# One plain copy of the transposed weights in place of a split into two rounded parts, in the second layer's attention

## The chip, the cores and the metric

The kernel runs on one core of a Trainium2 chip. The metric is the device time of one execution in microseconds (us), lower is better. A core has TensorE for matmuls (PE in the profile; its weight loads are listed as PEld), VectorE (DVE), ScalarE (ACT), GpSimd (POOL) and SyncE (SP), which here only starts DMAs. Matmuls write to PSUM banks; DVE and ACT read them.

## The reference, cut to what matters

The model is a two-layer decoder trunk over 1024 tokens of width 1024, all in float32. The first layer (A) has a sparse attention with three branches, the second (B) a dilated attention over shared keys and values; both end in a SwiGLU. The change is in layer B:

```python
DILATIONS = ((128, 1), (512, 4), (2048, 16))

def banded_attention(q, k, v, max_dist, dist_scale, rel_bias):
    ...
    s = jnp.einsum('nbqgrd,nbkgd->nbgrqk', qb, kw).astype(jnp.float32) * dh ** -0.5
    ...
    p, denom, m = masked_softmax(s + bias, mask[None, :, None, None])
    o = jnp.einsum('nbgrqk,nbkgd->nbqgrd', p, vw.astype(jnp.float32))
    o = o / denom[..., 0].transpose(0, 1, 4, 2, 3)[..., None]
    lse = (jnp.log(denom) + m)[..., 0].transpose(0, 1, 4, 2, 3).reshape(n, L, G, R)
    return o.reshape(n, L, G, R, dh), lse

def dilated_attention(h, w_q, k_shared, v_shared, w_out, rel_bias):
    q = (h @ w_q).reshape(B, S, N_DIL, N_KV, GQA_R, HEAD_DIM)
    ...  # one banded attention for each of the three dilations
    alpha = jax.nn.softmax(jnp.stack(lses, axis=-1), axis=-1)
    o = jnp.einsum('bsgrdi,bsgri->bsgrd', jnp.stack(outs, axis=-1), alpha)
    return o.reshape(B, S, D_MODEL).astype(h.dtype) @ w_out
```

There are 16 heads of 64 columns in 4 groups; the four heads of a group share their keys and values.

## The kernel before, in words

The program runs stage after stage: projections and attention of layer A, its output projection and feed-forward part, the projection of layer B's queries and of the shared keys and values (`project_B`), layer B's attention, and layer B's output projection and feed-forward part with the final norm. Within a stage, the order of the instructions in each engine's queue is set by a planner that simulates a timeline when the program is built; `after(...)` fixes single pairs. Each engine then takes its queue in order and waits on semaphores.

Numbers that need more than TensorE's quick rounded format (`F32R`, "fp32r" in the profile) are split: a rounded part on ACT (`split`, L165) and the rest on DVE (L166). A product of two such pairs takes two or three rounded matmuls. A matmul of two plain float32 operands needs no split.

`project_B` computes V for each of the three dilations, transposes it with TensorE, splits it, and stores for each token tile and group 128 columns: 64 of the rounded part and 64 of the rest (`vBs`). The stores are started by POOL.

Layer B's attention loops over the four groups. For each, `wide_job` is made for 8 residues r and two pairs of heads (hp 0 and 1): 64 units in all that do the dilations 4 and 16 together, with three blocks of 128 keys. `near_job` is made for 8 tiles t of 128 queries and two pairs: 64 units for dilation 1, with two blocks of keys (one at t = 0). Each is a `unit`. Its front part computes for the two heads e of its pair the scores into an `s` bank (L1672 and L1677, or L1692), adds the bias on DVE (L1638, with the row's minimum) and takes the exponential on ACT (L1643) into P. Its back part, `back`, is issued two units later (`pipelined(jobs(), 2)`): for at most two blocks at a time it transposes the weights of both heads into a `pt` bank (`transposed`, L328), brings them to SBUF, and multiplies them with V into an `o` bank (`mm_pv`). There are three `s`, three `pt` and two `o` banks.

How the transposed weights leave the `pt` bank differs before the change. Mostly they are split into th on ACT (L165) and tl on DVE (L166), 512 columns at a time. The third block of a wide unit (`pick`) is copied as traw by ACT for hp 0 and by DVE for hp 1 (L340), and split by POOL (L341, L342). For hp 1 of near units with an even tile (`unsplit`), the plain copy of ACT (L332) is used as it is.

`mm_pv` takes all 128 columns of V as weights, so the output rows 0 to 63 hold the product with V's rounded part and the rows 64 to 127 that with the rest, for 2 x 128 columns, the queries of the two heads. With th and tl these are two rounded matmuls (L348, L349) for each block; with traw it is one plain matmul (L347), of which the profile lists two records. After the second pair, `evac_o` adds the two halves: for each e, ACT copies one half of the rows (L359) and DVE adds the other to it (L360), and head e lands on the rows 64 e to 64 e + 63 of its destination, which is `o12` for wide units (every eighth column) and `oT` for near ones.

`merge` weighs and adds the two results of a group with small transposes (L1707, L1713, L1735) and matmuls with `crow` (L1742, L1743, L1744), spread between the units of the next stretch.

Of the kernel before, what the change touches and what calls it, by code (L numbers as in the profile page):

```python
# [10 lines left out]
F32 = mybir.dt.float32  # L11
F32R = mybir.dt.float32r
# [9 lines left out]
NT = S // 128  # L22
KC = D // 128
H = 16
G = 4
DH = 64
# [89 lines left out]
def trunk(ctx, tc, I, out):  # L116
    nc = tc.nc
# [7 lines left out]
    f32 = lambda ap: ap.bitcast(F32)  # L125
# [3 lines left out]
    dram = pool(ctx, "dram", space=DR)  # L129
# [10 lines left out]
    def bank(name):  # L140
        return psum[name].tile([128, 512], F32, name=name, bufs=BANKS.get(name, 1))
# [6 lines left out]
    ident = cst.tile([128, 128], F32, name="ident")  # L148
# [13 lines left out]
    def split(H_, L_, src, scale=None, eng=None):  # L162

        if scale is None:
            prev = nc.scalar.activation(H_, src, AF.Copy)  # L165
            rest = (eng or nc.vector).tensor_sub(L_, src, f32(H_))  # L166
            (on_vector if eng is None else on_pool)[0] = rest
        else:
            prev = nc.scalar.activation(H_, src, AF.Copy, scale=scale)
            nc.vector.scalar_tensor_tensor(L_, src, scale, f32(H_), op0=OP.mult, op1=OP.subtract)  # L170
        return prev
# [173 lines left out]
    def mm_pv(o_, v, th, tl, cs, first, last):  # L345
        if tl is None:
            return nc.tensor.matmul(o_, f32(v), th[:, cs], start=first, stop=last, skip_group_check=True)  # L347
        nc.tensor.matmul(o_, v, th[:, cs], start=first, stop=False, skip_group_check=True)  # L348
        return nc.tensor.matmul(o_, v, tl[:, cs], start=False, stop=last, skip_group_check=True)  # L349

    cp_a, cp_v = nc.scalar.copy, nc.vector.tensor_copy

    def evac_o(p, po, dst):

        ov = po[:].rearrange("p (c e q) -> p c e q", e=2, q=128)
        tmp = p.tile([128, 2, 128], F32, name="ot", bufs=2)
        for e in range(2):
            own, oth = slice(64 * e, 64 * e + 64), slice(64 - 64 * e, 128 - 64 * e)
            nc.scalar.activation(tmp[own], ov[oth, :, e, :], AF.Copy)  # L359
            nc.vector.tensor_add(dst[own], ov[own, :, e, :], tmp[own])  # L360
# [1027 lines left out]
    xS = dram.tile([S, D], F32, name="xS")  # L1388
    qB = dram.tile([3, H, 128, S], F32, name="qB")
    kBs = dram.tile([3, G, 2, DH, S], F32, name="kBs")  # L1390
    vBs = dram.tile([3, NT, 128, G, 128], F32, name="vBs")
    second = ("T1", "T2", "T3", "T4", "B22")

    def dense(layer, w, x_src, oT, tail, near, far):
# [29 lines left out]
    def project_B(c, B, xr, scratch):  # L1424
# [51 lines left out]
        def tokens_out(n):  # L1476

            i = jobs[n][1]
            got = {}

            def done(a, r, C):
                got[a, r] = C
                if (a, r) == (1, 0):
                    got[a, r] = (place if i == 2 else lambda x: x)(own("x1"))
                    nc.scalar.activation(got[a, r], view_of(n)(C[:]), AF.Copy)
                if (a, r) != (1, 1):
                    return
                banks = Turns(["dx0", "dx1", "dx2", "dx3"])
                for t in range(NT):
                    if i == 0:  # L1490
                        hf, cols = t // 4, lambda x: x[:, (t % 4) * 128:(t % 4 + 1) * 128]
                    elif i == 1:
                        hf, cols = t % 2, lambda x: x[:, t // 2:512:4]
                    else:
                        hf = t % 2
                        cols = lambda x: x.rearrange("p j r -> p r j")[:, t - hf:t - hf + 2, :] \
                            .rearrange("p r j -> p (r j)")
                    pt = bank(banks())
                    for s in range(2):
                        nc.tensor.transpose(pt[:, s * 128:(s + 1) * 128], cols(got[s, hf]), ident)  # L1500
                    vt = vts().bitcast(F32R).rearrange("p (g d) -> p g d", d=128)
                    split(vt[:, :, 0:64], vt[:, :, 64:128], pt[:, :256].rearrange("p (g d) -> p g d", d=64))
                    if i < 2:
                        nc.gpsimd.dma_start(vBs[i, t], f32(vt))
                    else:
                        for s in range(2):
                            nc.gpsimd.dma_start(vBs[i, t - hf + s, hf * 64:(hf + 1) * 64],
                                                f32(vt[s * 64:(s + 1) * 64]))
            return done

        def view_of(n):
# [45 lines left out]
    with ExitStack() as c:  # L1557
# [10 lines left out]
                nc.scalar.activation(crow[:, a * 512:(a + 1) * 512], rs_f, AF.Copy, scale=0.0)  # L1568
        rQ = [Ring(f"Q{i}", [128, S], F32R, [(bB if i == 0 else bA, 4)]) for i in range(3)]
        rK = [Ring(f"K{i}", [128, S], F32R, [(bB if i == 0 else bA, 2)]) for i in range(3)]  # L1570
        rV = [Ring(f"V{i}", [128, NT, 128], F32R, [(bB if i == 0 else bA, 1)]) for i in range(3)]
        rT0 = Ring("T0", [128, 256], F32, [(bB, 5)])
        rT12 = Ring("T12", [128, 384], F32, [(bA, 4), (bB, 4)])
        grp = {}
# [1 line left out]
        def load_first():  # L1576

            T = {}
            for i in (1, 2):
                T[i] = grp[i, 0] = [rQ[i].tile() for _ in range(4)], [rK[i].tile() for _ in range(2)], rV[i].tile()  # L1580
            for lo, hi in ((0, 256), (256, 512), (512, 1024)):
                for i in (1, 2):
                    Q, K, V = T[i]
                    for hh in range(4):
                        nc.sync.dma_start(f32(Q[hh][:, lo:hi]), qB[i, hh][:, lo:hi])
                    if hi > 512 and i == 1:
                        continue
                    ks = slice(2 * lo, 2 * hi) if i == 1 else slice(lo + 128 * (lo > 0), min(hi + 128, S))
                    for z in range(2):
                        for b in range(2):  # L1590
                            nc.sync.dma_start(f32(K[z][b * 64:(b + 1) * 64, ks]), kBs[i, 0, z][:, ks])
                    vs = slice(ks.start // 128, ks.stop // 128)
                    nc.sync.dma_start(f32(V[:, vs]), vBs[i, vs, :, 0, :].rearrange("t p d -> p t d"))

        def load(i, g):
            Q = [rQ[i].tile() for _ in range(4)]
            K = [rK[i].tile() for _ in range(2)]
            V = rV[i].tile()
            for hh in range(4):
                nc.sync.dma_start(f32(Q[hh]), qB[i, 4 * g + hh])  # L1600
                if hh == 0:
                    for z in range(2):
                        load_k(K[z], kBs[i, g, z])
            nc.sync.dma_start(f32(V), vBs[i, :, :, g, :].rearrange("t p d -> p t d"))
            grp[i, g] = Q, K, V

        def load_T12(g, e):
# [17 lines left out]

        po_ = {}

        pick = lambda hp, b0, nb: (cp_a, cp_v)[hp] if nb == 3 and b0 == 2 else None
        unsplit = lambda key, hp: key[1] == 0 and hp == 1 and key[2] % 2 == 0

        def unit(key, hp, stats, slot, score, bias, n, blocks, dst):

            P = wk.tile([128, 2, 384], F32, name="P", bufs=4)
            for e in range(2):
                hh = 2 * hp + e
                ps = bank("s")
                score(ps, hh)
                nc.vector.tensor_tensor_reduce(out=P[:, e, :n], in0=ps[:, :n], in1=bias(hh), scale=1.0,  # L1638
                                               scalar=3e38, op0=OP.add, op1=OP.min,
                                               accum_out=stats[:, slot, hh:hh + 1])  # L1640
            for e in range(2):
                hh = 2 * hp + e
                nc.scalar.activation(P[:, e, :n], P[:, e, :n], AF.Exp, bias=stats[:, slot, hh:hh + 1], scale=-1.0,  # L1643
                                     accum_out=stats[:, slot, 4 + hh:5 + hh])

            def back():
                if hp == 0:
                    po_[key] = bank("o"), None
                po, prev = po_[key]
                nb = len(blocks)  # L1650
                for b0 in range(0, nb, 2):
                    bs = range(b0, min(b0 + 2, nb))
                    th, tl = transposed(wk, [P[:, e, b * 128:(b + 1) * 128] for b in bs for e in range(2)],
                                        pick(hp, b0, nb), 5, unsplit(key, hp))
                    for i, b in enumerate(bs):
                        cs = slice(i * 256, (i + 1) * 256)
                        o_ = po[:, hp * 256:(hp + 1) * 256]
                        with after(prev if b == 0 else None):
                            prev = mm_pv(o_, blocks[b], th, tl, cs, b == 0, b == nb - 1)
                po_[key] = po, prev  # L1660
                if hp == 1:
                    evac_o(wk, po, dst)
            return back

        def wide_job(g, r, hp):
# [178 lines left out]
```

## Time and profile before

| | |
|---|---|
| three runs | 2938.28 us median, 2936.68 to 2944.49 |
| the profiled execution | 2938.84 us, of which its span is 2937.1 |
| granted TensorE clock over the span | 0.989 |
| PE busy | 2816.6 us (96%) |
| DVE busy | 2398.0 us (82%) |
| ACT busy | 1621.1 us (55%) |
| POOL busy | 1642.7 us (56%) |
| layer B's attention | about 1857 to 2180 us of the span |

A row of a group has line, engine, operation, out and in by the program's names, shapes, and the count; then the busy time in us with the mean of one in ns; then the idle time of the engine just before, and what ended it ("<-"; "issue" where nothing that the profile shows was waited for). A row of the timeline has the start and the length in us. Matmuls are pipelined: a matmul's length includes the way through the array and out of it, and the next starts before its end. A shape such as 128*64 with 128x64 stands for 128 rows and 64 columns of weights and 64 columns that stream through. A row of the table by stretches gives each engine's busy time and count, the granted clock, and the share of the DMA engines.

### The profile page before, as it was taken

The page shows a single profiled execution, that of the slowest core. Times are in us where ns is not written, and L with a number is a line of the kernel's source. Part 1 is how long each engine was busy: PE and PEld are TensorE (multiplying, and loading weights), DVE is VectorE, ACT ScalarE, POOL GpSimd, SP SyncE. Part 2 cuts the span into 40 slices and gives each one's busy share as a digit, 9 for nine tenths or more (in the row PEclk, how much of TensorE's full clock was granted, in tenths as well). Part 3 has the DMA queues.
Part 4 walks back from the last instruction along what each step waited for, and adds up shares of the span by engine and source line. Part 5 has one row for each costly group of instructions (what it writes and reads, how often), then busy time and mean ns, then how long its engine had stood idle before and what let it go on. Part 6 is the DMA issues. An engine that isn't in the chain of part 4 may idle for free. (4 is left out here: it accounts for less than half of the span.)

```text
span 2937.1 us, 44584 instructions
## 1 busy us (share of the span) xinstructions
PE 2816.6 (96%) x14734; PEld 2375.5 (81%) x14734; DVE 2398.0 (82%) x4866; ACT 1621.1 (55%) x3615; POOL 1642.7 (56%) x1727
## 2 busy tenths in 40 slices
PE   9999999999999999999999999899989999999997
PEld 8888888887778888888777778788867788888886
DVE  5543988988888989989976777699998788888887
ACT  5432988887563433334454444699975543343334
POOL 3135766765566556556547777444425655666562
PEclk9999999999999999999999999999999999999999
DMA  8678132112322222231225555865431211112112
GB/s 255 212 240 296 34 105 82 44 47 80 108 62 65 71 73 69 62 85 52 84 85 153 155 162 148 278 201 164 136 136 52 69 57 59 58 47 65 54 44 76
DMA packets 277319, 317.59 MB, mean 108 GB/s; under 512 B 19196, under 2 KB 210733, under 8 KB 277088
## 3 DMA queue, kind: packets, MB, share of 16 engines
q1 hardware_dynamic: 255344, 246.50, 27.8%
q0 software_dynamic: 21744, 68.23, 7.4%
q8 instruction: 117, 1.92, 0.3%
q14 instruction: 114, 0.93, 0.1%
HBM read 243.17 MB, written 87.20 MB: 112 GB/s over the span
## 5 line engine op out<-in xcount | busy, mean ns | idle before, releaser
L885 DVE TENSOR_TENSOR pl<-oT,ph 128x512 fp32r<-128x512 f32 x337 | 350.8, 1058 | 57.5 <-PE dr L934 17.4
L884 ACT ACTIVATE ph<-oT 128x512 fp32r<-128x512 f32 x347 | 210.9, 626 | 203.7 <-PE ux L1082 54.6
L328 PE MATMUL pt<-ident,P 128*128 128x128 f32 x1536 | 243.7, 276 | 11.0 <-DVE tl L166 5.3
L166 DVE TENSOR_TENSOR tl<-pt,th 128x512 fp32r<-128x512 f32 (+1 forms) x336 | 217.5, 653 | 27.2 <-ACT th L165 25.7
L884 ACT ACTIVATE ph<-oTb 128x512 fp32r<-128x512 f32 x239 | 145.6, 627 | 170.4 <-PE ux L1082 52.9
L885 DVE TENSOR_TENSOR pl<-oTb,ph 128x512 fp32r<-128x512 f32 x233 | 213.2, 937 | 28.9 <-PE dr L934 17.4
L939 DVE TENSOR_TENSOR xr<-xr,dr 128x512 f32<-128x512 f32 x320 | 204.0, 679 | 15.9 <-PE dr L934 15.4
L803 POOL TENSOR_SCALAR P<-P,sm,gates 128x384 f32<-128x384 f32 (+7 forms) x256 | 183.4, 728 | 44.8 <-DVE sm L801 39.7
L939 DVE TENSOR_TENSOR xr<-xr,dx 128x512 f32<-128x512 f32 x320 | 204.6, 678 | 1.9 <-PE dx L934 1.9
L165 ACT ACTIVATE th<-pt 128x512 fp32r<-128x512 f32 (+1 forms) x336 | 185.6, 565 | 35.6 <-PE pt L328 31.0
L328 PEld LDWEIGHTS pt<-ident,P 128*128 128x128 f32 x1536 | 178.7, 141 | 32.0 <-DVE tl L166 5.3
L1266 POOL TENSOR_TENSOR oT<-oT,gffn 128x512 f32<-128x512 f32 x92 | 113.5, 1244 | 139.7 <-DMA oT<-in_ffn_w_up_dram 101.8
L799 ACT ACTIVATE P<-P,m 128x384 f32<-128x384 f32 (+7 forms) x256 | 170.7, 669 | 9.0 <-DVE m L797 7.2
L1266 POOL TENSOR_TENSOR oTb<-oTb,gffn 128x512 f32<-128x512 f32 x92 | 109.7, 1199 | 99.6 <-DMA oTb<-in_ffn_w_up_dram 69.1
L349 PE MATMUL o<-tl,V 128*128 128x256 f32 x572 | 159.1, 300 | 6.4 <-POOL tl L342 2.8
L348 PE MATMUL o<-th,V 128*128 128x256 f32 x572 | 159.8, 298 | 3.7 <-DVE o L360 2.2
L341 POOL TENSOR_SCALAR th<-traw 128x256 fp32r<-128x256 f32 x112 | 95.7, 854 | 105.9 <-DVE traw L340 40.2
L1643 ACT ACTIVATE P<-P,st 128x384 f32<-128x384 f32 (+2 forms) x256 | 139.7, 548 | 7.7 <-DVE st L1638 6.4
L1638 DVE CUSTOM_DVE_ANT_0 P<-s,T 128x384 f32<-128x384 f32 (+2 forms) x256 | 114.8, 476 | 12.8 <-PE s L1677 4.6
L349 PEld LDWEIGHTS o<-tl,V 128*128 128x128 f32 x572 | 108.6, 190 | 16.5 <-DVE tl L166 11.0
L348 PEld LDWEIGHTS o<-th,V 128*128 128x128 f32 x572 | 108.9, 190 | 12.4 <-DVE o L360 5.3
L884 ACT ACTIVATE ph<-wd 128x512 fp32r<-128x512 f32 x86 | 53.6, 627 | 99.8 <-PE ux L1082 48.5
(642 smaller groups left out, 9096.1 us busy)
## 6 DMA issues: line engine op xcount, KB each, us to landing
qB<-xr POOLq DMA_DIRECT2D x96, 256.0 KB, 4.6
oT<-in_ffn_w_up_dram SPq DMA_DIRECT2D x92, 256.0 KB, 2.9
oTb<-in_ffn_w_up_dram SPq DMA_DIRECT2D x92, 256.0 KB, 2.9
Q<-qB SPq DMA_DIRECT2D x40, 512.0 KB, 5.8
wd<-in_ffn_w_down_dram SPq DMA_DIRECT2D x66, 256.0 KB, 2.5
oT<-in_b_w_q_dram SPq DMA_DIRECT2D x48, 256.0 KB, 4.5
K<-kBs SPq DMA_DIRECT2D x40, 256.0 KB, 8.6
wraw<-in_a_w_in_dram SPq DMA_DIRECT2D x18, 512.0 KB, 7.4
```

The lines of the kernel that those rows point to most:

```text
L165: prev = nc.scalar.activation(H_, src, AF.Copy)
L166: rest = (eng or nc.vector).tensor_sub(L_, src, f32(H_))
L328: nc.tensor.transpose(ps[:, i * 128:(i + 1) * 128], b, ident)
L348: nc.tensor.matmul(o_, v, th[:, cs], start=first, stop=False, skip_group_check=True)
L349: return nc.tensor.matmul(o_, v, tl[:, cs], start=False, stop=last, skip_group_check=True)
L799: nc.scalar.activation(P[:, e, :n], P[:, e, :n], AF.Exp, bias=mm[:, e:e + 1], scale=-1.0, accum_out=sm[:, e:e + 1])
L803: nc.gpsimd.tensor_scalar(P[:, e, :n], P[:, e, :n], sm[:, e:e + 1], gt(g, t, br, 2 * hp + e, 1), op0=OP.mult, op1=OP.mult)
L884: nc.scalar.activation(h, src, AF.Copy)
L885: (eng or nc.vector).tensor_sub(l, src, f32(h))
L939: nc.vector.tensor_add(xs, xs, banks[t])
L1266: nc.gpsimd.tensor_mul(v, v, gains[:, k:k + 4].unsqueeze(2).to_broadcast([128, 4, 128]))
L1643: nc.scalar.activation(P[:, e, :n], P[:, e, :n], AF.Exp, bias=stats[:, slot, hh:hh + 1], scale=-1.0, accum_out=stats[:, slot, 4 + hh:5 + hh])
```

## The change

Layer B's V is no longer split: `project_B` copies the transposed V (one ACT copy) and stores 64 plain columns for each group, so `vBs` and the rings of V in SBUF have half the width. In `back`, both heads' transposed weights are copied once and as they are (`turned_heads`): by DVE for the third block of the wide units and for hp 1 of the near units, else by ACT. POOL has no part in it any more. `pv_heads` multiplies plain values: for each block and each head one matmul with the 64 columns of V as weights and the head's 128 columns of queries; head e's output goes to the rows 64 e to 64 e + 63 of the `o` bank, in the columns of its pair. `evac_o` is replaced by one DVE copy of 128 rows and 256 columns. Layer A keeps `transposed`, `mm_pv` and `evac_o`.

```diff
+    def turned_heads(p, blocks, copy):
+        ps = bank("pt")
+        for i, b in enumerate(blocks):
+            nc.tensor.transpose(ps[:, i * 128:(i + 1) * 128], b, ident)
+        w = len(blocks) * 128
+        t = p.tile([128, 512], F32, name="pT", bufs=5)
+        copy(t[:, :w], ps[:, :w])
+        return t
+
+    def pv_heads(po, hp, v, pT, first, last):
+        for e in range(2):
+            prev = nc.tensor.matmul(po[64 * e:64 * e + 64, hp * 128:(hp + 1) * 128], v, pT[:, e * 128:(e + 1) * 128],
+                                    start=first, stop=last, skip_group_check=True)
+        return prev
...
-    vBs = dram.tile([3, NT, 128, G, 128], F32, name="vBs")
+    vBs = dram.tile([3, NT, 128, G, DH], F32, name="vBs")
...
-                    vt = vts().bitcast(F32R).rearrange("p (g d) -> p g d", d=128)
-                    split(vt[:, :, 0:64], vt[:, :, 64:128], pt[:, :256].rearrange("p (g d) -> p g d", d=64))
+                    vt = vts()[:, :256]
+                    nc.scalar.copy(vt, pt[:, :256])
+                    vt = vt.rearrange("p (g d) -> p g d", d=DH)
                     if i < 2:
-                        nc.gpsimd.dma_start(vBs[i, t], f32(vt))
+                        nc.gpsimd.dma_start(vBs[i, t], vt)
...
-        rV = [Ring(f"V{i}", [128, NT, 128], F32R, [(bB if i == 0 else bA, 1)]) for i in range(3)]
+        rV = [Ring(f"V{i}", [128, NT, DH], F32, [(bB if i == 0 else bA, 1)]) for i in range(3)]
...
-        pick = lambda hp, b0, nb: (cp_a, cp_v)[hp] if nb == 3 and b0 == 2 else None
-        unsplit = lambda key, hp: key[1] == 0 and hp == 1 and key[2] % 2 == 0
...
-                    th, tl = transposed(wk, [P[:, e, b * 128:(b + 1) * 128] for b in bs for e in range(2)],
-                                        pick(hp, b0, nb), 5, unsplit(key, hp))
+                    copy = nc.vector.tensor_copy if b0 == 2 or key[1] == 0 and hp == 1 else nc.scalar.copy
+                    pT = turned_heads(wk, [P[:, e, b * 128:(b + 1) * 128] for b in bs for e in range(2)], copy)
                     for i, b in enumerate(bs):
-                        cs = slice(i * 256, (i + 1) * 256)
-                        o_ = po[:, hp * 256:(hp + 1) * 256]
                         with after(prev if b == 0 else None):
-                            prev = mm_pv(o_, blocks[b], th, tl, cs, b == 0, b == nb - 1)
+                            prev = pv_heads(po, hp, blocks[b], pT[:, i * 256:(i + 1) * 256], b == 0, b == nb - 1)
                 po_[key] = po, prev
                 if hp == 1:
-                    evac_o(wk, po, dst)
+                    nc.vector.tensor_copy(dst, po[:, :256].rearrange("p (c q) -> p c q", q=128))
```

More of the change, by code (lines that the diff above doesn't have):

```diff
@@ L1507, in done @@
                             nc.gpsimd.dma_start(vBs[i, t - hf + s, hf * 64:(hf + 1) * 64],
-                                                f32(vt[s * 64:(s + 1) * 64]))
+                                                vt[s * 64:(s + 1) * 64])
             return done
@@ L1592, in load_first @@
                     vs = slice(ks.start // 128, ks.stop // 128)
-                    nc.sync.dma_start(f32(V[:, vs]), vBs[i, vs, :, 0, :].rearrange("t p d -> p t d"))
+                    nc.sync.dma_start(V[:, vs], vBs[i, vs, :, 0, :].rearrange("t p d -> p t d"))
         def load(i, g):
@@ L1603, in load @@
                         load_k(K[z], kBs[i, g, z])
-            nc.sync.dma_start(f32(V), vBs[i, :, :, g, :].rearrange("t p d -> p t d"))
+            nc.sync.dma_start(V, vBs[i, :, :, g, :].rearrange("t p d -> p t d"))
             grp[i, g] = Q, K, V
```

## The prediction

> **What bounds the kernel now.** I read the page first for the engines over the whole span, then the table by stretches for the stage that the change touches, then the groups of that stage by form, and last the timeline, for the pace at which TensorE (PE) takes each kind of matmul.
>
> ```profile
> span 2937.1 us, 44584 instructions
> ...
> PE 2816.6 (96%) x14734; PEld 2375.5 (81%) x14734; DVE 2398.0 (82%) x4866; ACT 1621.1 (55%) x3615; POOL 1642.7 (56%) x1727
> ...
> core 0: us, PE busy (x) PEld busy (x) DVE busy (x) ACT busy (x) POOL busy (x), PEclk, DMA share, GB/s
> 1857.00:2180.00 323.00, 294.58 (x2162) 263.09 (x2161) 290.16 (x908) 291.30 (x840) 127.30 (x163) 0.99 0.58 175
> 1950.00:2000.00 50.00, 48.06 (x370) 43.62 (x370) 47.48 (x147) 45.97 (x134) 26.09 (x32) 1.00 0.61 180
> ```
>
> Layer B's attention is the stretch from 1857 to 2180 us: 323 us, a ninth of the span. Three engines look equally full there (PE 295, VectorE (DVE) 290, ScalarE (ACT) 291 us). For DVE and ACT that is real work: they run one instruction at a time. For PE it is not, since a matmul's row lasts from its start to the end of its pipeline and the next one starts earlier. So PE's demand has to be counted by start-to-start paces.
>
> ```profile
> 1964.65 0.82 PE L328 MATMUL pt<-ident,P 128*128 128x128 f32 x6
> ...
> 2016.99 0.28 PE L348 MATMUL o<-th,V 128*128 128x256 f32 x1
> ...
> 2017.58 0.28 PE L349 MATMUL o<-tl,V 128*128 128x256 f32 x1
> 2014.15 1.02 PE L347 MATMUL o<-traw,V 128*128 128x256 f32 x4
> ```
>
> ```profile
> L328 PE MATMUL pt<-ident,P 128*128 128x128 f32 x624 | 101.2, 280 | 7.5 <-DVE tl L166 4.1 <-DVE o L1743 2.0 <-ACT ot L359 0.4
> L348 PE MATMUL o<-th,V 128*128 128x256 f32 x284 | 81.1, 307 | 3.7 <-DVE o L360 2.2 <-DVE oTb L360 1.1
> L349 PE MATMUL o<-tl,V 128*128 128x256 f32 x284 | 78.1, 297 | 3.1 <-POOL tl L342 2.8
> L347 PE MATMUL o<-traw,V 128*128 128x256 f32 x56 | 14.7, 378 | 0.0
> ```
>
> Six transposes take 0.82 us, the last of them 0.28: (0.82 - 0.28) / 5 = 0.108 us each. From the matmul at 2016.99 to the one at 2017.58 are five steps of rounded matmuls with 256 columns: 0.118 us each. The plain ones of L347 leave two records per product; four records in 1.02 us, the last 0.38: 0.214 us per record, so 0.43 us for a plain product with 256 columns, or 0.107 per 128 columns and record. The stage's demand on PE is then: 624 transposes x 0.108 = 67 us; 568 rounded products with V x 0.118 = 67; 56 plain records x 0.214 = 12; the scores, by the code 128 x 4 + 128 x 2 = 768 rounded ones, of which 736 have 256 columns, at the same 0.118 = 87, and 32 half of that = 2; the rest of the 2162 records, some 150 (merge, next stage), at an estimated 0.14 = 21. Sum 256 us, 79% of the stage. DVE and ACT, at 90%, hold it, and PE has some 34 us before it reaches DVE's load.
>
> **The change, engine by engine, in this stage.** Blocks of keys: wide units (64) have three, near units have two except at the first tile: 64 x 3 + 2 x 4 x 15 = 312. Before, 284 of them run as th and tl, 28 plain.
>
> ```profile
> L166 DVE TENSOR_TENSOR tl<-pt,th 128x512 fp32r<-128x512 f32 x108 | 73.6, 684 | 5.6 <-ACT th L165 5.1
> L360 DVE TENSOR_TENSOR o<-o,ot 64x256 f32<-64x256 f32 x64 | 41.3, 646 | 3.6 <-ACT ot L359 2.6
> L360 DVE TENSOR_TENSOR oTb<-o,ot 64x256 f32<-64x256 f32 x64 | 26.9, 420 | 2.5 <-ACT ot L359 1.1
> L340 DVE COPY traw<-pt 128x256 f32<-128x256 f32 x32 | 13.5, 420 | 4.8 <-PE pt L328 4.1 <-issue 0.4
> L165 ACT ACTIVATE th<-pt 128x512 fp32r<-128x512 f32 x108 | 63.7, 592 | 8.0 <-PE pt L328 6.8
> L359 ACT ACTIVATE ot<-o 64x256 f32<-64x256 f32 x128 | 48.5, 379 | 10.2 <-PE o L349 2.7 <-DVE oTb L360 2.5 <-PE o L347 1.7
> L340 ACT COPY traw<-pt 128x256 f32<-128x256 f32 x32 | 11.6, 364 | 5.1 <-PE pt L328 3.7 <-POOL tl L342 1.3
> L332 ACT COPY traw<-pt 128x512 f32<-128x512 f32 x12 | 6.9, 574 | 0.0
> L341 POOL TENSOR_SCALAR th<-traw 128x256 fp32r<-128x256 f32 x64 | 54.7, 855 | 60.2 <-DVE traw L340 37.5 <-ACT traw L340 20.3 <-PE o L349 0.7
> L342 POOL TENSOR_TENSOR tl<-traw,th 128x256 fp32r<-128x256 f32 x64 | 46.9, 738 | 3.7
> ```
>
> *DVE.* Leaves: 73.6 + 41.3 + 26.9 + 13.5 = 155 us. Comes: 64 copies of 256 columns (the third block of the wide units) x 0.420 = 27; 28 copies of 512 for near units with hp 1 at L166's 0.684 = 19, and four short ones = 2; 64 evacuations of one plain copy: the 32 near ones at 0.420 = 13, the 32 wide ones, which write the same strided rows as the 0.646 form, between 0.420 and 0.646, I take 0.55 = 18. That is 79; DVE falls from 290 to about 214 us.
>
> *ACT.* Leaves: 63.7 + 48.5 + 11.6 + 6.9 + 3 (short forms) = 134. Comes: 92 copies of 512 at 0.592 and four short ones = 56. ACT falls from 291 to about 213.
>
> *POOL* loses 54.7 + 46.9 = 102 us. It isn't late anywhere here, so nothing is counted for that.
>
> *PE, products.* Leaves 67 + 12 = 79 us; 177 stay. Comes: 312 blocks x 2 heads x 2 records = 1248 records of 128 columns. Upper end, one after another: 1248 x 0.107 = 134 us, 0.43 per block. Lower end, if the two heads, on different halves of the output rows, run side by side: half, 67 us. No row shows two halves at work together. In between: weights seem to be loaded one matmul ahead (the rows of L533 below: a load of 64 columns takes about 0.055). A head's second record and the next head's first could then start 0.055 apart instead of 0.107, and a block takes 2 x 0.107 + 2 x 0.055 = 0.32, 101 us in all. I take the middle of 67 and 101, 84 us, because the two records of a head must follow one another and the records of different heads need not. By the Trainium skill's page "TensorEngine Tiling (Array Packing)", section Key Properties, different tiles load and multiply in parallel; by it the products would take the lower end, which is the second rival below.
>
> *PE, switches.* The new products have 64 output rows. One place of this trace already has such a form between full ones:
>
> ```profile
> 201.79 0.39 PE L205 MATMUL mm<-hH,wl 128*128 128x512 f32 x1
> 202.02 0.39 PE L203 MATMUL mm<-hH,wh 128*128 128x512 f32 x1
> 202.34 0.19 PEld L533 LDWEIGHTS cmp<-w2t,hid 128*64 128x64 f32 x2 [0.35 <-issue]
> 202.34 0.33 PE L533 MATMUL cmp<-w2t,hid 128*64 128x64 f32 x2
> 202.59 0.19 PEld L204 LDWEIGHTS mm<-hL,wh 128*128 128x128 f32 x1
> 202.60 0.50 PE L204 MATMUL mm<-hL,wh 128*128 128x512 f32 x1
> 202.94 0.39 PE L205 MATMUL mm<-hH,wl 128*128 128x512 f32 x1
> L533 PE MATMUL cmp<-w2t,hid x16: 222/222/270, 202.3 to 204.3; 128*64 128x64 f32 x16
>   issue: 0.7, 2
> ```
>
> L203 starts at 202.02 and streams for 0.23 (the step from 201.79), until 202.25. The load of L533 begins only at 202.34, with nothing named that it waited for ("issue", twice), and its second matmul starts at 202.34 + 0.33 - 0.22 = 202.45 where 202.30 was possible: 0.15 lost. On the way back the array is free at about 202.50, and L205 starts at 202.94 where 202.73 was possible: 0.2 lost. So a run of narrow products costs about 0.35 us at its two borders; where transposes follow, whose weights load faster, about 0.29. The same stands behind the eight-row transposes of the merge:
>
> ```profile
> 1916.75 0.66 PE L1713 MATMUL pt<-ident,mrow 8*128 8x8 f32 x8 [0.25 <-ACT mrow L1708]
> ...
> 1917.34 0.50 PE L1692 MATMUL s<-K,Q 128*128 128x256 f32 x2
> ...
> L1713 PE MATMUL pt<-ident,mrow 8*128 8x8 f32 x32 | 2.6, 204 | 1.8 <-ACT mrow L1708 1.8
> ```
>
> The last of the eight starts at 1916.75 + 0.66 - 0.20 = 1917.21, and the next only 0.13 later, though their step is 0.46 / 7 = 0.066. The same page and section of the Trainium skill says that a change of the tiling mode drains the engine; the trace agrees with these 0.15 and 0.2. In this stage every run of products stands between transposes and scores, which are full. 128 units make 192 groups of products; the wide units' two groups will often be neighbours (their six transposes are, in the first timeline row above), and some units merge. I take 140 runs x 0.32 = 45 us; ends 100 x 0.29 = 29 and 192 x 0.35 = 67.
>
> *The stage.* PE: 177 + 84 + 45 = 306 us, against 214 and 213 of DVE and ACT. PE becomes the bound. How a bound turns into time I take from DVE now: in a full stretch it is busy 47.48 of 50 us, 95%; so its 290 fill 305 us, and 18 of the 323 are at the edges (first loads, last merge). 306 / 0.95 + 18 = 340, 17 us more than now. An evacuation now waits for PE alone instead of PE and ACT; behind it on DVE stand the next scores' reductions, and PE's own next scores wait for those through the three s banks, so a late run of products delays PE a second time, which the 0.95 is to hold.
>
> *Elsewhere.* In the projection ahead of the stage, 24 splits of V lose their DVE half, and V's DMAs (as many as before) carry half the bytes.
>
> ```profile
> L166 DVE TENSOR_TENSOR oT<-dx,oT 128x256 fp32r<-128x256 f32 x24 | 9.8, 419 | 11.9 <-ACT oT L165 11.9
> 1520.00:1610.00 90.00, 86.23 (x390) 70.24 (x390) 56.20 (x74) 43.52 (x76) 60.33 (x74) 0.98 0.47 145
> V<-vBs SPq DMA_DIRECT2D x10, 512.0 KB, 5.6
> ```
>
> DVE has 56 of 90 us there and PE 86, so the 9.8 us were covered by PE's work; if that cover is less than it looks, 2 us come back. V's loads land in 5.6 us and sit on SP's queue far ahead of their use; at the first group, half a megabyte less may let the stage begin 1 us earlier, and the shorter runs per packet may eat that. Together I take -1, ends 0 and -4.
>
> Sum: 2938.84 us, the profiled execution's own time, + 17 - 1 = 2955; that execution is 0.6 above the median of the runs, 2938.28, which I neglect. A difference under about 0.3% (9 us) can't be told from none here.
>
> **Rivals.**
>
> *Side by side doesn't happen.* For it: the plain products of the trace (L347) follow one another strictly, and the two heads share one bank. Then PE has 177 + 134 + 45 = 356, the stage 393, +70: 3008 us. Against it: the two halves touch neither each other's weights nor each other's rows.
>
> *Side by side in full:* the products take 67 us. PE then has 177 + 67 + 45 = 289, the stage 322, the time 2937, no change. For it: nothing in the code ties one head's half to the other's. Against it: no row shows two matmuls at work at once, and L533's loads follow one matmul ahead, not more. This is what the Trainium skill's page "TensorEngine Tiling (Array Packing)", section Key Properties, would give.
>
> *The switches cost nothing here* (the one that ends faster): the borders fall where PE would stand waiting for a copy anyway, as now at "DVE tl". Then PE has 177 + 84 = 261 us, the stage is 261 / 0.95 + 18 = 293, -30: 2908 us; with the products at 67, 2890. For it: PE has 67 idle us now, and its waits of today go with the splits. Against: once PE is the bound it has few such waits. It decides once products and switches together are under about 113 us, for then PE is under DVE's 290 of today; I have 129.
>
> *The order stays as it is and something else holds the stage:* two o banks, three banks of scores, and the exponentials that feed the transposes. Then the stage stays within a few us, 2930 to 2947.
>
> **How the numbers follow.** Forecast 0.37, 2955, its own range 2936 (products 67) to 2980 (products 101, 160 runs); of it 0.32 are slower by more than 0.3%, 0.05 within. Strictly one after another 0.22, all slower. Side by side in full 0.10: 0.07 within, 0.03 faster. No cost of switches 0.25, all faster. Another hold 0.06, all within. That gives faster 0.28, same 0.18, slower 0.54. The range reaches from the faster rival to the slower one, 2898 to 3012: outside are the tails of both.
>
> **What would show it.** In the changed kernel's trace: DVE near 214 and ACT near 213 us of busy time in the stage, and idle times in front of both ended by PE; 1248 records of the form 128*64 with 128 columns streaming, and their step: 0.05 alternating with 0.107 if side by side, 0.107 throughout if not; the load after each border about 0.13 after the last start, put down to "issue". The forecast is wrong if the stage is shorter than 315 us, if the records' step is 0.107 throughout, or if the runs of products number far from 140. All of it assumes that the order, which is planned anew for the changed program, still puts scores and transposes between most runs.

## The result, and the profile after

| | before | after |
|---|---|---|
| median of four runs on one chip | 2937.98 us (2936.68 to 2944.49) | 2919.64 us (2917.50 to 2924.46) |
| ratio to before | | 0.9935, 95% interval 0.9916 to 0.9955 |
| span of the profiled execution | 2937.1 us | 2919.4 us |
| granted clock over the span | 0.989 | 0.989 |
| stage, first score to last product | 1856.1 to 2176.4: 320.3 us | 1854.0 to 2159.3: 305.3 us |
| one group of four, in the steady part | 76.2 us | 73.7 us |

The change is faster by 18.3 us; slower had been forecast. The spans differ by 17.7: 15.0 lie inside the stage, 2.1 ahead of it and 0.6 behind it. The time of one group is the distance in the trace between points a quarter of the product records apart. Four groups of 73.7 are 295; the other 10 us of the stage are its edges (before: 320.3 - 4 x 76.2 = 15.5).

The page after, in the same lines as before: PE's share went up, that of the other three down.

```profile
span 2919.4 us, 45291 instructions
...
PE 2823.7 (97%) x15358; PEld 2358.6 (81%) x15358; DVE 2312.0 (79%) x4730; ACT 1550.2 (53%) x3423; POOL 1539.5 (53%) x1599
```

The table by stretches after, for the stage, for the 50 us shown of before, and for 100 us in the middle:

```profile
core 0: us, PE busy (x) PEld busy (x) DVE busy (x) ACT busy (x) POOL busy (x), PEclk, DMA share, GB/s
1854.00:2159.30 305.30, 299.50 (x2782) 242.50 (x2781) 224.09 (x792) 216.62 (x643) 25.30 (x34) 0.99 0.60 176
1950.00:2000.00 50.00, 50.00 (x482) 40.13 (x483) 34.50 (x133) 36.77 (x112) 0.00 (x0) 1.00 0.56 163
1950.00:2050.00 100.00, 100.00 (x947) 81.12 (x946) 72.42 (x256) 71.06 (x211) 6.66 (x8) 1.00 0.55 162
```

DVE went from 290 to 224 us and ACT from 291 to 217 (214 and 213 were forecast). PE is busy without a gap. That alone proves no bound, since its rows overlap; its waits and its demand, counted below, decide. The groups of the stage by form, after:

```profile
L355 PE MATMUL pt<-ident,P 128*128 128x128 f32 x624 | 107.8, 285 | 0.0
L365 PE MATMUL o<-pT,V 128*64 128x128 f32 x1248 | 104.4, 287 | 1.1 <-ACT pT L358 1.1
...
L358 ACT COPY pT<-pt 128x512 f32<-128x512 f32 x92 | 52.7, 574 | 35.3 <-PE pt L355 35.3
...
L358 DVE COPY pT<-pt 128x256 f32<-128x256 f32 x68 | 28.8, 423 | 43.4 <-ACT P L1659 17.7 <-PE pt L355 15.6 <-ACT pT L358 6.7
...
L1676 DVE COPY o<-o 128x256 f32<-128x256 f32 x32 | 20.7, 647 | 3.4 <-PE o L365 3.2
L358 DVE COPY pT<-pt 128x512 f32<-128x512 f32 x28 | 19.0, 680 | 3.3 <-PE pt L355 2.3 <-ACT P L1659 0.9
L1676 DVE COPY oTb<-o 128x256 f32<-128x256 f32 x32 | 13.4, 420 | 7.4 <-PE o L365 7.2
```

In 1248 products and 624 transposes PE stood idle 1.1 us; the copies now wait for PE ("PE pt L355", 35.3 us on ACT). The chain of the stage after is PE to 85%, with the products of L365 first; loads and their issue are most of the rest:

```profile
by line: PE o L365 27.8%; PE pt L355 25.0%; PE s L1706 9.7%; PE s L1686 8.7%; PE s L1691 8.5%; PE pt L1756 2.8%; SPq L1610 2.8%; SPq L1604 2.5%; DMA K<-kBs 2.4%; DMA ow<-in_b_w_out_dram 2.0%; PE pt L1749 1.2%; PE pt L1721 1.0%; SPq L1612 0.
```

Now the products' pace. The timeline of PE after, with start and length in us:

```profile
1960.27 0.40 PE L1691 MATMUL s<-K,Q 128*128 128x256 f32 x2
1960.60 0.44 PE L365 MATMUL o<-pT,V 128*64 128x128 f32 x4
1960.96 0.66 PE L355 MATMUL pt<-ident,P 128*128 128x128 f32 x4
1961.38 0.48 PE L1686 MATMUL s<-K,Q 128*128 128x256 f32 x2
...
1962.03 0.88 PE L365 MATMUL o<-pT,V 128*64 128x128 f32 x12
```

Twelve records take 0.88 us with the last one's 0.27. In the trace's single records, the two heads' matmuls start 0.006 apart, the next pair 0.109 later: a pair takes the time of one. So 1248 records are 624 pairs x 0.109 = 68 us. The Trainium skill, page "TensorEngine Tiling (Array Packing)", section Key Properties, says that different tiles load and multiply in parallel; the trace agrees with these 0.006 us.

The borders are in the same rows. The second score of 1960.27 starts at 1960.39; the first narrow product could follow at 1960.50 and starts at 1960.60. Its second pair comes 0.16 behind the first and not 0.109, for that pair's load began only 0.05 behind the first product. From the last narrow pair to the next transpose are again 0.20 where 0.10 would do, and the second transpose comes 0.17 behind the first where 0.109 would do. The loads show it as idle time that ends with "issue", here in the timeline of PE's weight loads:

```profile
1960.59 0.20 PEld L365 LDWEIGHTS o<-pT,V 128*64 128x64 f32 x4
1960.96 0.42 PEld L355 LDWEIGHTS pt<-ident,P 128*128 128x128 f32 x4 [0.17 <-issue]
```

Where scores follow a run, the second of them comes 0.22 behind the first (0.50 less the last one's 0.28) and not 0.12, so such a run loses about 0.35 us; 18 of the runs are of this kind:

```profile
2142.95 0.66 PE L365 MATMUL o<-pT,V 128*64 128x128 f32 x8
2143.54 0.50 PE L1706 MATMUL s<-K,Q 128*128 128x256 f32 x2
```

Over the 161 runs of products (counted in the order of the records) the loss is 0.296 us a run, 48 us in the stage. The same section of the Trainium skill's page says that a change of the tiling mode drains the engine. The trace agrees with it by the delays at the two changes, 0.09 us ahead of a run and 0.10 behind it; the other two stand inside the runs, behind loads that started late.

PE's demand in the stage is then: 244.4 us for all records at their paces (products 68, all else 176), and 48.8 for 165 borders (161 runs, and four runs of the merge's eight-row transposes). That is 293.2, or 73.3 in each group, and a group takes 73.7: 99.5%.

### The profile page after: what moved, and what is told of

It is laid out like the page before. It is cut to its first block, busy times and chain, and to the rows that moved or that the text cites. A ratio compares the mean times of both kernels' runs of the same rounds, so it can differ in the third digit from the quotient of the medians.

```text
span 2919.4 us, 45291 instructions
## 1 busy us (share of the span) xinstructions
PE 2823.7 (97%) x15358; PEld 2358.6 (81%) x15358; DVE 2312.0 (79%) x4730; ACT 1550.2 (53%) x3423; POOL 1539.5 (53%) x1599
## 4 chain that ended last, share of the span: by engine, by line
PE 75%; DVE 12%; ACT 4%; DMA 3%; issue 2%; POOL 2%; SPq 1%; DVEq 0%; ACTq 0%; POOLq 0%
PE ux L1100 17%; PE uy L1100 14%; PE dx L952 7%; PE dr L952 5%; PE dr L1100 3%; PE o L365 3%; PE pt L355 3%; PE mm L204 2%; PE mm L203 2%; PE mm L205 2%; DVE P L811 2%; DVE pl L903 2%; PE pt L328 2%; DVE tl L166 1%; PE dx L1100 1%
## 5 line engine op out<-in xcount | busy, mean ns | idle before, releaser
L166 DVE TENSOR_TENSOR tl<-pt,th 128x512 fp32r<-128x512 f32 (+1 forms) x224 | 142.0, 641 | 23.3 <-ACT th L165 22.1
L328 PE MATMUL pt<-ident,P 128*128 128x128 f32 x912 | 144.3, 276 | 3.5 <-DVE cd L745 1.2
L165 ACT ACTIVATE th<-pt 128x512 fp32r<-128x512 f32 (+1 forms) x224 | 120.1, 554 | 31.8 <-PE pt L328 24.2
L328 PEld LDWEIGHTS pt<-ident,P 128*128 128x128 f32 x912 | 108.1, 142 | 14.2 <-DVE tl L166 3.3
L1640 POOL TENSOR_SCALAR_AFFINE_SELECT T<-T 128x256 f32<-128x256 f32 x16 | 6.1, 400 | 195.9 <-DMA T<-sA 73.3
L952 PE MATMUL dx<-ph 128*128 128x512 f32 x320 | 107.5, 390 | 1.3 <-ACT ph L902 1.3
L355 PE MATMUL pt<-ident,P 128*128 128x128 f32 x624 | 107.8, 285 | 0.0
L952 PE MATMUL dx<-ph,pl 128*128 128x512 f32 x320 | 107.0, 389 | 0.0
L365 PE MATMUL o<-pT,V 128*64 128x128 f32 x1248 | 104.4, 287 | 1.1 <-ACT pT L358 1.1
```

The source lines that it names most:

```text
L328: nc.tensor.transpose(ps[:, i * 128:(i + 1) * 128], b, ident)
L355: nc.tensor.transpose(ps[:, i * 128:(i + 1) * 128], b, ident)
L365: prev = nc.tensor.matmul(po[64 * e:64 * e + 64, hp * 128:(hp + 1) * 128], v, pT[:, e * 128:(e + 1) * 128], start=first, stop=last, skip_g ...
L952: nc.tensor.matmul(banks[t], part(a, t)[u], b[v], start=z == 0 and onX != 2, stop=z == 2, skip_group_check=True)
```

## The experiments

Each ran three rounds against the kernel before on the same chip (medians of before 2937.2 to 2938.7), and ratios are to it. "Demand" is PE's, counted as above, for one group.

**One half of the rows.** Both heads' products go to rows 0 to 63, the second head's to other columns of the bank. It does not compute the reference; the instructions and their sizes are as in the changed kernel, but for the evacuation in two copies.

```diff
-po[64 * e:64 * e + 64, hp * 128:(hp + 1) * 128]
+po[0:64, e * 256 + hp * 128:e * 256 + hp * 128 + 128]
...
-nc.vector.tensor_copy(dst, po[:, :256]...)
+nc.vector.tensor_copy(dst[0:64], po[0:64, :256]...)
+nc.scalar.copy(dst[64:128], po[0:64, 256:512]...)
```

> Both heads' products go to rows 0 to 63 (head 1 in the bank's other columns); ACT copies head 1's half to its rows, which adds 64 short copies (24 us) to ACT. Theory A (PE is the bound of the changed stage, and its products are as cheap as they are because the two heads run side by side): the 1248 records then follow one another at 0.109 us, 136 us instead of 68; with 175 runs of products in the planned order instead of 161 (0.3 us each) the stage grows by about 72 us, to 2990 us. Rival B (the gain came from DVE and ACT alone, PE has room): 2920 to 2925 us. Steps between the records: A 0.109 throughout, no pairs at 0.006.

Measured 2991.7 us (2989.0 to 2995.2), ratio 1.0183 (1.0167 to 1.0198). The timeline of its PE shows a run of twelve:

```profile
2000.23 1.52 PE L366 MATMUL o<-pT,V 128*64 128x128 f32 x12
```

1.52 us against 0.88: every record is 0.109 behind the one before it. The time is 72 us above the changed kernel's: 1248 x 0.109 - 68 = 68 for the products, and 14 more runs (175) x 0.296 = 4. So the two halves of the rows are worth about 70 us, and without them the change would have lost 53 us, where the prediction's "side by side doesn't happen" has 70.

**The copy alone.** The kernel before, with its weights copied once and plain; V stays as two parts of 64 columns and `evac_o` adds the halves, so that each product is a plain one of full width.

```diff
-th, tl = transposed(wk, [...], pick(hp, b0, nb), 5, unsplit(key, hp))
+copy = nc.vector.tensor_copy if b0 == 2 or key[1] == 0 and hp == 1 else nc.scalar.copy
+th, tl = turned_heads(wk, [...], copy), None
```

> The kernel before with one part of the change alone: the transposed weights are copied once by the engines that the changed kernel uses, and multiplied plain; V keeps its two stored parts as 128 columns of weights, and the two halves are added as before. 312 blocks x 0.43 us = 134 us of products, no narrow runs. Theory A: PE has 177 + 134 = 311 us and holds the stage at about 323, so 2938 us, no gain at all from the copies. Rival B: DVE (about 258 us) and ACT (265 us) fall as far below 290 as they do here, so the stage goes with them, to about 290 us or 2905 to 2915 us. Step of the plain records 0.215 throughout.

Measured 2954.2 us (2948.8 to 2956.0), ratio 1.0049 (1.0031 to 1.0066): slower than before by 16. Half of the change loses, though DVE and ACT became lighter, which refutes the rival. The first theory is 16 too low: a group takes 81.0 us with a demand of 77.6, 96%, and the stage takes 336 us where it has 323. The stage also begins 4 us later than before, at 1860.4; why, the trace does not settle.

This kernel has plain products of full width between scores and transposes, and they pay no border: in its records the first one starts 0.119 behind a score and the next transpose 0.216 behind the last one, each at its own pace. So it is the 64 columns that cost at the borders, and not the change of format.

**More transposes, in each kernel.** The transposes of the first pair of heads are made twice, 312 more of 0.109 us: 34 us of PE's time that no other engine shares.

```diff
-for i, b in enumerate(blocks):
+for i, b in list(enumerate(blocks)) * times:
...
+times = 2 - hp
```

Before, so changed:

> The kernel before, with the transposes of each pair's first unit made twice into the same bank: 312 transposes more, 34 us of PE, nothing more for DVE or ACT. If DVE and ACT held the stage before and PE had room (256 of 320 us), the time grows by 0 to 12 us, to 2938 to 2950. If PE held it already, by 34, to 2972.

Measured 2951.9 us, ratio 1.0042 (1.0030 to 1.0055): 14.8 of the 34 us. After, so changed:

> The same doubling in the changed kernel: 34 us of PE, and the planned order has 174 runs instead of 161, 4 us. Theory A (PE alone holds the changed stage, 99% full): all of it shows, 2957 us. Rival B (PE has room there too): 2920 to 2932.

Measured 2955.0 us, ratio 1.0059 (1.0041 to 1.0076): 35.4 above the changed kernel, all of it (and it has 13 runs more). A group takes 83.1 us with a demand of 82.8. So after the change PE alone holds the stage. Before it, neither theory is quite right: PE was neither the bound nor free. The tables by stretches, first of before with more transposes, then of after with more:

```profile
1950.00:2050.00 100.00, 97.09 (x766) 90.02 (x766) 90.95 (x277) 86.30 (x250) 45.28 (x56) 1.00 0.50 146
```

```profile
1950.00:2050.00 100.00, 100.00 (x923) 81.85 (x922) 67.11 (x231) 63.83 (x184) 9.23 (x10) 1.00 0.46 133
```

In the first DVE is at 91% and PE's demand at 72.5 of 79.3 us, 91% too, and neither fills up.

**Before with light copies.** The kernel before, with one rounded copy in place of both parts, used for both products, and the halves not added: the low part and the addition are left out. PE keeps its 568 rounded full-width products, makes 56 more such in place of the plain ones, and has no narrow runs.

```diff
-th, tl = transposed(wk, [...], pick(hp, b0, nb), 5, unsplit(key, hp))
+th = tl = turned_heads(wk, [...], copy)   # one F32R copy
...
-evac_o(wk, po, dst)
+nc.vector.tensor_copy(dst, po[:, :256]...)
```

> The kernel before with the changed kernel's load on DVE and ACT: one rounded copy of the transposed weights, multiplied twice (the low part is left out), and one DVE copy of the bank in place of the addition of its halves (also left out). All products have 128 rows, so there are no narrow runs. PE has 177 + 624 x 0.118 = 251 us, DVE and ACT about 214 and 213. If a stage in which PE alone is near full runs at 99.5% of PE's load plus 10 us at the edges, as the changed kernel does, the stage is 262 us and the time about 2877. If the 95% of the kernel before belongs to the stage itself, 274 to 282 us and 2889 to 2897.

Measured 2886.7 us (2886.0 to 2888.0), ratio 0.9826 (0.9810 to 0.9843). A group takes 64.0 with a demand of 62.6, 98%; before, it took 76.2 with a demand of 64.0, 84%. PE's work is 1.4 us a group lighter, 6 in the stage; the rest of the 52 us comes with the lighter load of the other engines, and with a shorter way from transpose to product (one copy in place of ACT's part and then DVE's). This kernel does not tell the two apart. Its time lies between the theories, 10 us above the first one's number and 2 under the second one's range; its share, 98%, is nearer to the first. Its table by stretches:

```profile
1950.00:2050.00 100.00, 99.57 (x852) 97.78 (x851) 82.35 (x311) 83.04 (x254) 6.66 (x8) 1.00 0.71 207
```

**After with heavy copies.** Every copy of pT is made twice.

```diff
 copy(t[:, :w], ps[:, :w])
+copy(t[:, :w], ps[:, :w])
```

> The changed kernel with each copy of transposed weights made twice on its engine, into the same place: DVE about 272, ACT about 270 us in the stage, PE 293 + 5 (179 runs in the planned order). If PE holds the stage at 99.5% whatever the others do, 310 us, time 2925. If it is the nearness of three engines that costs, as in the kernel before (95%), 324 us, time 2938.

Measured 2940.9 us, ratio 1.0002 (0.9992 to 1.0012), as the second theory had it. A group takes 78.5 us (the one before it 77.0), PE's demand (18 more borders) is 74.6: 95 to 97%.

```profile
1950.00:2050.00 100.00, 96.96 (x876) 75.83 (x875) 79.91 (x271) 80.91 (x225) 9.16 (x10) 1.00 0.47 133
```

So PE falls from 99.5 to 95 or 97% when DVE and ACT rise from 72 and 71 to 80 and 81 of 100 us. Whether their load does it or the copies' longer way between transpose and product, the time does not tell apart, for the kernel changes both. The trace leans to the load: from 1900 to 2120 us PE stood idle 5.3 us, 3.2 of them with scores that waited for DVE's reductions, 1.5 in the merge and 0.6 with products that waited for a copy; the changed kernel has no such idle time there. Waits shorter than the overlap of two matmul rows do not show in these sums.

**Fewer borders.** PE's order is written by hand: scores of unit u, transposes of u - 2, and the products of both units of a pair together, so that two units make one run. pT has 8 buffers.

```diff
+if u >= 2: turn(u - 2)
+if u >= 5 and u % 2: mult(u - 5); mult(u - 4)
```

> The changed kernel with PE's order in this stage written out: scores of a unit, transposes of the unit two before, and the products of both units of a pair in one run, two pairs behind. 63 runs of products instead of 161. Theory A with borders at 0.30 us: 98 fewer runs are 29 us less for PE, 264 us, the stage about 276 to 283, 2891 to 2898 us. Rival C (the borders hide in waits): 2920 us. If the fixed order makes PE wait for copies or banks, the loss shows as idle time of PE ended by ACT or DVE.

Measured 2906.9 us (2905.5 to 2909.4), ratio 0.9894 (0.9880 to 0.9909), 63 runs. The same written order with each unit's products in a run of their own, 125 runs (`if u >= 4: mult(u - 4)`):

> The same written order with the products of each unit in a run of their own, right behind the transposes of the unit two before: 125 runs. Theory A: 62 runs more than with joined runs, 18 to 19 us more than it, about 2910 us. Rival C: the same time as the joined one within 3 us.

Measured 2922.3 us (2918.8 to 2924.4), ratio 0.9945 (0.9930 to 0.9959). The pair differs in the grouping, and so in how long half of the products wait for their turn: 15.4 us for 62 runs, 0.25 us a run (0.27 by the stages, 308.2 and 291.7). So the borders are real time on PE. Less than their price comes back: here most runs have scores behind them (43 of 63 and 96 of 125), which makes about 0.33 us a run and 21 us for the 62. DVE and ACT are a little fuller in the shorter kernel, but no run shows that this is the reason. In the timeline of the loads of the joined kernel each border stands alone:

```profile
1942.33 1.29 PEld L365 LDWEIGHTS o<-pT,V 128*64 128x64 f32 x24 [0.17 <-issue]
1943.79 0.30 PEld L1689 LDWEIGHTS s<-K,Q 128*128 128x128 f32 x2 [0.17 <-issue]
```

They came out 9 to 16 and 12 us above what was expected. A written order can't go round a late operand, and at the start PE of the joined kernel stands behind K's loads, 7.5 us in all where the changed kernel has 3.3:

```profile
1863.72 0.35 PE L1689 MATMUL s<-K,Q 128*128 128x256 f32 x1 [3.54 <-DMA K<-kBs]
...
1867.56 0.55 PE L1694 MATMUL s<-K,Q 128*128 128x256 f32 x1 [2.70 <-DMA K<-kBs]
```

**Fewer borders, the rest free.** Only scores, transposes and products keep the written order, from the ninth unit on; the first units and the merge are placed by the planner. 68 runs.

> Joined runs as in the run before, but only scores, transposes and products keep the written order, from the ninth unit on; the merge's matmuls and the first units are left to the planner. 68 runs of products. PE's demand is 244 + 68 x 0.3 = 264 us. If the earlier written order lost its time to merges and first loads, the stage is 276 to 282 us and the time 2890 to 2897 us; if the joined order itself makes PE wait for copies, 2907 us as before.

Measured 2903.4 us (2902.0 to 2904.5), ratio 0.9879 (0.9863 to 0.9895): about 34 us under before and 16 under the changed kernel, the fastest here that computes the whole reference. A group takes 68.2 us with a demand of 66.4, 97%. It ended between the two theories, 6 us above the first one's range; the 3 us that came back are within the intervals of the two ratios.

**Head by head.** The products of a unit's group are queued as both blocks of head 0, then both of head 1, so that partners are two matmuls apart in the queue.

```diff
-for i, b in enumerate(bs):
-    pv_heads(...)          # head 0, head 1 of block i
+for e in range(2):
+    for i, b in enumerate(bs):
+        nc.tensor.matmul(po[64 * e:64 * e + 64, ...], blocks[b], ...)
```

> The changed kernel with the products of a group in another order: both blocks of head 0, then both of head 1, in place of block by block with the heads in turn. If PE takes matmuls strictly as queued, 4 records of one half and then 4 of the other share only one step: 7 steps in place of 4 in the 124 groups of two blocks, 40 us more, 2960 us. If it looks ahead over four records, the pairs at 0.006 stay and the time is 2920.

Measured 2919.8 us (2919.6 to 2921.2), ratio 0.9936 (0.9920 to 0.9951), the same as the changed kernel. A run of twelve in the timeline of its PE:

```profile
1962.54 0.88 PE L1674 MATMUL o<-pT,V 128*64 128x128 f32 x12
```

0.88 us, as above; partners start 0.013 apart instead of 0.006. Records on one half start 0.109 apart (as in the kernel with one half), so partners are of different heads. So PE starts head 1's matmuls ahead of head 0's second one, which stands before them in the queue.

## Why the prediction was wrong

**The step that failed first is the conversion of demand into time,** "306 / 0.95 + 18". The 95% was DVE's in the stage of before, where DVE and ACT were both that full and PE's demand at 84%. After the change one engine was left, and it ran at 99.5% of its demand; the edges were 10 us and not 18. With the prediction's own 306 this gives 306 / 0.995 + 10 = 318 in place of 340, 22 us. The runs that show it: the changed kernel, one half of the rows (99.4%) and more transposes after (99.6%) have one full engine; heavy copies bring the same kernel back to 95 or 97%, and light copies bring before from 84 to 98%. The second delay that the 0.95 was to hold, scores that wait for DVE's reductions through the s banks, does not show after the change in the steady part (no idle time of PE from 1900 to 2120 us); with heavy copies it does (3.2 us). The kernels side by side:

| kernel | PE's demand of a group | a group | share | DVE, ACT busy in 100 us |
|---|---|---|---|---|
| before | 64.0 | 76.2 | 84% | 94, 91 |
| before, more transposes | 72.5 | 79.3 | 91% | 91, 86 |
| copy alone | 77.6 | 81.0 | 96% | 80, 80 |
| after, heavy copies | 74.6 | 78.5 | 95% | 80, 81 |
| before, light copies | 62.6 | 64.0 | 98% | 82, 83 |
| joined | 66.1 | 69.4 | 95% | 77, 75 |
| joined, the rest free | 66.4 | 68.2 | 97% | 78, 75 |
| runs apart | 70.6 | 73.1 | 97% | 74, 71 |
| after | 73.3 | 73.7 | 99.5% | 72, 71 |
| after, more transposes | 82.8 | 83.1 | 99.6% | 67, 64 |
| one half of the rows | 91.4 | 91.9 | 99.4% | 64, 69 |

By and large, the more room the others have, the nearer PE comes to its demand. It is no function of the two shares alone: the light copies are at 98% beside 82 and 83, the runs apart at 97% beside 74 and 71. Part of that is the price: the table counts every border at 0.296, and with 0.35 where scores follow, the three written orders come to 96% (joined), 98% (the rest free) and 98% (apart). That the load of the others sets the share is thus argued from these kernels side by side; none changes the load and nothing else.

**The products were mis-sized:** 84 us taken, 68 measured, 16 us. The pace of 0.055 that L533's loads seemed to set is not there: the loads of both halves start 0.006 apart as well. The middle between 67 and 101 was chosen for want of a row; the argument against full overlap, that L533's loads follow one matmul ahead, came from a form that uses one half alone.

**The borders held:** 45 us taken, 48 measured. There are 161 runs and not 140, which adds 6 us, at 0.296 us and not 0.32, which takes 3 back. Both prices read off L533's single place in layer A, 0.29 where transposes follow and 0.35 otherwise, were right within 0.01.

Together: 340 - 22 - 16 + 3 = 305, the stage as measured. Elsewhere -2.7 came where -1 was taken, and the stage of before, as counted, is 320.3 and not 323.

**What was right:** PE becomes the bound; what stays of its work (177 taken, 176 counted); DVE and ACT within 10 and 4 us. DVE's 10 come from the reading that it runs one instruction at a time: its rows overlap. Added up, they fell from 346 to 271 us, by 75 where 76 were forecast (the wide evacuation, 0.647 us where 0.55 was taken, is made up elsewhere); but 56 us of them overlapped before and 47 after, so its busy time fell by 66.

**The rivals.** "Side by side in full" had the mechanism, and its time, 2937, was wrong by the same conversion: its 289 us of demand give 289 / 0.995 + 10 = 301. "Switches cost nothing" gave the sign, with 2890 to 2908 us, 12 or more under the result, and for a reason that the joined kernels refute: they cost 48 us. That it named the right side was luck. That something else holds the stage is excluded by the 35.4 us that more transposes cost after the change. Rounded, the ledger of the stage is: PE's demand from 256 to 293 (products 79 to 68, borders 0 to 49), and the time in which PE had nothing to do from 64 us to 12; net -15.

## What to carry to other kernels

In these kernels PE came the nearer to its demand (from 84 to 99.6%) the more room DVE and ACT had, with exceptions of some per cent. So take the share from a stretch where as many engines are near full as will be after the change, and not from the engine that bounds now. Where a change takes load from two of three nearly full engines, most of the third one's idle time can come back (52 of 64 us here), even if its own work grows. Narrow matmuls on the two halves of the output rows run in pairs at the price of one, but each run of them between full ones pays 0.30 to 0.35 us here, so group the runs before counting the gain.

## What the runs showed of the hardware that was not expected

Two matmuls with 64 columns of weights on different halves of the output rows start 0.006 us apart and cost as one, loads too; on one half they cost two (0.88 against 1.52 us for twelve records).

PE does not start matmuls in the order of its queue when they are on different halves: in the kernel that queues head by head, partners two matmuls apart start 0.013 us apart, and the time is 2919.8 against 2919.6 us. The Trainium skill's page "TensorE: Matmul & The Clock Gate", Part 3, has matmuls start and end strictly in order; the measurement differs for this form, and it decides.

A run of narrow products pays at four places: 0.09 us ahead of the first pair, 0.05 between first and second, 0.10 behind the last, and between the two full matmuls that follow 0.06 if they are transposes and 0.10 if they are scores. The first three are nearly the same beside transposes and beside scores.

What stays open: why the copy alone begins its stage 4 us later than before (the light copies do too), why the written orders reach 96 to 98% and not 99.5%, and how much of the 3 to 5% that PE loses with heavy copies is the load and how much the length of the copies' way.
